# First layer of a four-layer trunk: VectorE in the source's order, the weighting placed behind the next unit's first maxima, the products with v in one piece

## The chip, the cores and the metric

The kernel runs on one core of a Trainium2 chip. The metric is device microseconds of one execution, the median of several runs. All inputs lie in device memory when the time starts, and the output is written back within it.

## What is computed

Four layers over x (256 positions, 1024 channels, float32): a layer normalizes its input, mixes positions, multiplies with a gate, projects and adds a normalized result to its input. The change is in layer 0, "native sparse attention". Its core, cut from the reference:

```python
q, kc, vc, ks, vs, kw, vw, gl, z = split_cols(u @ w_in, A_SPLITS)      # 16 heads, 4 kv heads, 64 wide
kcmp = compress(kc, pos_k, w1_k, w2_k)       # gelu(blk @ w1) @ w2, 15 blocks of 32 positions
vcmp = compress(vc, pos_v, w1_v, w2_v)
p_c = masked_softmax(q @ kcmp - slopes * dist, dist >= 0);   o_c = p_c @ vcmp
p_s = masked_softmax(q @ ks - slopes * dist, causal);        o_s = p_s @ vs
p_w = masked_softmax(q @ kw - slopes * dist, causal);        o_w = p_w @ vw
o = sum(sigmoid(gl) * [o_c, o_s, o_w])       # a gate per head and branch
return (o * silu(z)) @ w_out
```

With 256 positions the selection takes all blocks and the window holds all positions, so the selected and the window branch are both plain causal attention.

## The kernel before, in words

**Split weights.** Products with the weights are done in a reduced float32 format in three matmuls: a weight tile is loaded raw (L83, SyncE's queue, 5 raw buffers), ScalarE copies its high part (L104), VectorE subtracts to get the low part (L106), and TensorE adds high by high, low by high and high by low (L200 to L202, or L260 to L262 in the output projection). `advance` (L69) issues loads and splits as far as buffers allow: 11 split tiles may live at a time, and the low part follows the high part at once in the program.

**Queues.** TensorE's order is that of the source throughout, with other engines ordered by the scheduler, by priorities and a model of the times. In the opening of layer 0 the source orders the other engines too, but not from there on.

**Filling.** A projection is a list of 16 steps of three matmuls, kept in a queue `fq`. `fill` (L208) pops some steps after every slot of attention work, so that TensorE has projection work between the pieces; how many is the rest of the queue less `keep`, over the slots left, rounded up.

**Layer 0 from the compression on.** `compress` (L651) does the first layer of the compression with 64 matmuls (L655), 4 steps of the first q projection behind every quarter; then comes the gelu (L665 to L669), the second layer (L686), and the projections of q for kv heads 1 to 3 (L636 keeps q and its low part, L644) and of the four gate pieces z (L392 to L395, L351, and a split for the output projection, L356 to L360). The 16 heads are 8 units of two; two units make a group that shares a kv head. For each group `cmp_front` (L729) has TensorE score the compressed keys (L736), VectorE reduce, mask, scale and subtract the maximum (L740 to L751), ScalarE take the exponential (L752) and VectorE normalize (L753 to L758); `cmp_back` (L760) transposes. A unit (L767) scores both branches for the first 128 positions in two S tiles (L785, L786), for the last 128 in two more, with two S buffers in all, which the compressed scores use as well. For each tile and branch VectorE adds the mask, takes the row's maximum (L294) and ScalarE the exponential (L296). When all are there, VectorE weights the P tiles with the gate over the sum (L797 to L807); then TensorE transposes them (L301) and multiplies with v (L317, L320), and adds the compressed branch (L819).

**Order of the slots.** `pipeline` (L368) runs the front of a unit against the back of the one before by a pattern, FFBFBBB: compressed scores (first unit of a group), first and second scores, `finish` with the last scores and the weighting, between them transposes of each branch and the products of each branch as slots of their own. Every slot is followed by a fill.

## Time and profile before

| | us |
|---|---|
| median of 3 runs | 581.33 (580.71 to 584.76) |
| the profiled execution | 583.38 |
| its span, first to last instruction | 581.7 |
| TensorE busy in the span | 560.6 (96%) |
| VectorE busy | 420.3 (72%) |
| ScalarE busy | 334.5 (58%) |
| mean granted clock of TensorE | 0.992 of full speed |

In the profile PE is TensorE (its ends are modelled, and matmuls overlap), PEld its weight loads, DVE VectorE, ACT ScalarE, POOL GpSimd, SP SyncE. A tile name stands for all its buffers: S are the score tiles, mm the projections, whi and wlo the split weights, cs the compressed scores, cm and cl their maxima and sums, la the sums of a unit. "Idle before, releaser" is the time that the engine stood still before an instruction and what ended it. The stretch that the change touches runs from about 48 us to the first output projection matmul at 165 us.

### The profile page before, as it was taken

The page shows a single profiled execution, that of the slowest core. Times are in us where ns is not written, and L with a number is a line of the kernel's source. Part 1 is how long each engine was busy: PE and PEld are TensorE (multiplying, and loading weights), DVE is VectorE, ACT ScalarE, POOL GpSimd, SP SyncE. Part 2 cuts the span into 40 slices and gives each one's busy share as a digit, 9 for nine tenths or more (in the row PEclk, how much of TensorE's full clock was granted, in tenths as well). Part 3 has the DMA queues.
Part 4 walks back from the last instruction along what each step waited for, and adds up shares of the span by engine and source line. Part 5 has one row for each costly group of instructions (what it writes and reads, how often), then busy time and mean ns, then how long its engine had stood idle before and what let it go on. Part 6 is the DMA issues. An engine that isn't in the chain of part 4 may idle for free.

```text
span 581.7 us, 10475 instructions
## 1 busy us (share of the span) xinstructions
PE 560.6 (96%) x3930; PEld 496.8 (85%) x3930; DVE 420.3 (72%) x947; ACT 334.5 (58%) x715; POOL 40.7 (7%) x89
## 2 busy tenths in 40 slices
PE   7999987989999999999999999999999999999995
PEld 6998876777788799999988789999987898888984
DVE  5973898887836896777974886768548778888632
ACT  6752787776824475676642474658524765666410
POOL 1900000000000100000420100000001000000000
PEclk9999998999999999999999999999999999999998
DMA  8774925521250596443352568443525683332002
GB/s 296 247 251 146 319 71 190 168 90 44 74 179 4 180 330 231 147 145 126 120 171 73 181 238 302 149 145 110 177 76 181 233 307 137 120 110 74 1 37 73
DMA packets 27779, 90.96 MB, mean 156 GB/s; under 512 B 4560, under 2 KB 5200, under 8 KB 27728
## 3 DMA queue, kind: packets, MB, share of 16 engines
q1 hardware_dynamic: 26144, 86.09, 43.7%
q10 hardware_dynamic: 1584, 4.20, 2.2%
q8 instruction: 31, 0.51, 0.4%
q14 instruction: 20, 0.16, 0.1%
HBM read 89.22 MB, written 1.05 MB: 155 GB/s over the span
## 4 chain that ended last, share of the span: by engine, by line
PE 81%; DVE 8%; issue 4%; ACT 2%; DMA 2%; POOL 1%; SPq 0%; POOLq 0%; DVEq 0%; ACTq 0%
PE mm L200 16%; PE mm L201 14%; PE mm L202 14%; PE mm L262 6%; PE mm L260 6%; PE mm L261 6%; PE pt L301 3%; DVE wlo L106 3%; PE S L311 3%; PE o L317 2%; ACT whi L104 1%; PE o L655 1%; DVE P L294 1%; DMA h<-in_x_dram 1%; PE pt L188 1%
## 5 line engine op out<-in xcount | busy, mean ns | idle before, releaser
L200 PE MATMUL mm<-uth,whi 128*128 128x256 f32 x736 | 219.0, 298 | 0.0
L106 DVE TENSOR_TENSOR wlo<-raw,whi 128x1024 fp32r<-128x1024 f32 (+1 forms) x153 | 182.3, 1207 | 43.4 <-ACT whi L104 42.8
L201 PE MATMUL mm<-utl,whi 128*128 128x256 f32 x736 | 208.5, 283 | 0.0
L202 PE MATMUL mm<-uth,wlo 128*128 128x256 f32 x736 | 208.3, 283 | 0.0
L104 ACT ACTIVATE whi<-raw 128x1024 fp32r<-128x1024 f32 (+1 forms) x153 | 157.0, 1043 | 73.5 <-PE mm L201 38.5
L200 PEld LDWEIGHTS mm<-uth,whi 128*128 128x128 f32 x736 | 140.9, 191 | 15.5 <-issue 14.7
L201 PEld LDWEIGHTS mm<-utl,whi 128*128 128x128 f32 x736 | 141.1, 192 | 0.9
L202 PEld LDWEIGHTS mm<-uth,wlo 128*128 128x128 f32 x736 | 140.9, 191 | 0.0
L260 PE MATMUL mm<-whi,qT 128*128 128x512 f32 x128 | 50.5, 394 | 0.0
L261 PE MATMUL mm<-whi,kT 128*128 128x512 f32 x128 | 49.9, 390 | 0.0
L262 PE MATMUL mm<-wlo,qT 128*128 128x512 f32 x128 | 49.9, 390 | 0.0
L260 PE MATMUL mm<-whi,uth 128*128 128x512 f32 (+1 forms) x112 | 42.6, 380 | 0.0
L262 PE MATMUL mm<-wlo,uth 128*128 128x512 f32 (+1 forms) x112 | 42.1, 376 | 0.0
L261 PE MATMUL mm<-whi,utl 128*128 128x512 f32 (+1 forms) x112 | 42.1, 376 | 0.0
L294 DVE CUSTOM_DVE_ANT_0 P<-S,mask 128x128 f32<-128x128 f32 (+1 forms) x96 | 30.6, 353 | 8.3 <-PE S L786 6.0
L415 ACT ACTIVATE junk<-mm 128x512 bf16<-128x512 f32 x16 | 9.5, 595 | 42.1 <-PE mm L262 42.1
L296 ACT ACTIVATE P<-P,mxa 128x128 f32<-128x128 f32 (+1 forms) x64 | 28.4, 447 | 3.7 <-DVE mxa L294 3.7
L146 ACT ACTIVATE PT<-pt 128x384 f32<-128x384 f32 x58 | 25.8, 483 | 7.5 <-PE pt L301 7.5
L262 PEld LDWEIGHTS mm<-wlo,qT 128*128 128x128 f32 x128 | 24.0, 188 | 5.0
L260 PEld LDWEIGHTS mm<-whi,qT 128*128 128x128 f32 x128 | 24.1, 188 | 4.7
L261 PEld LDWEIGHTS mm<-whi,kT 128*128 128x128 f32 x128 | 24.1, 188 | 4.7
L301 PE MATMUL pt<-ident,P 128*128 128x128 f32 x180 | 27.0, 279 | 0.5 <-DVE P L806 0.4
(207 smaller groups left out, 757.3 us busy)
## 6 DMA issues: line engine op xcount, KB each, us to landing
raw<-in_a_t_dram SPq DMA_DIRECT2D x24, 512.0 KB, 4.8
raw<-in_b_t_dram SPq DMA_DIRECT2D x24, 512.0 KB, 4.6
raw<-in_d_t_dram SPq DMA_DIRECT2D x24, 512.0 KB, 4.5
raw<-in_c_t_dram SPq DMA_DIRECT2D x20, 512.0 KB, 5.2
raw<-in_w_dram SPq DMA_DIRECT2D x8, 512.0 KB, 4.7
raw<-in_a_o_dram SPq DMA_DIRECT2D x8, 512.0 KB, 3.8
raw<-in_b_v_dram SPq DMA_DIRECT2D x8, 512.0 KB, 3.4
raw<-in_b_o_dram SPq DMA_DIRECT2D x8, 512.0 KB, 3.5
```

The source lines that it names most:

```text
L104: ACT.activation(hi, t, AF.Copy)
L106: lo_of = (POOL if on_pool else DVE).tensor_tensor(lo, t, hi.bitcast(F32), op=OP.subtract)
L146: ACT.activation(dst, src, AF.Copy)
L200: PE.matmul(o, sh, mh, start=first, stop=False)
L201: PE.matmul(o, sh, ml, start=False, stop=False)
L202: PE.matmul(o, sl, mh, start=False, stop=last)
L260: PE.matmul(o, sh, wh[:, j, c0:c1], start=k == 0, stop=False)
L261: PE.matmul(o, sl, wh[:, j, c0:c1], start=False, stop=False)
L262: PE.matmul(o, sh, wl[:, j, c0:c1], start=False, stop=k == 7)
L294: DVE.tensor_tensor_reduce(out=P[:, c0:c1], in0=S, in1=mask[:, c0:c1], scale=-slope, scalar=BIG, op0=OP.add, op1=OP.min, accum_out=mx)
L296: ACT.activation(P[:, c0:c1], P[:, c0:c1], AF.Exp, bias=mx, scale=-1.0, accum_out=l)
L301: PE.transpose(pt[:, i, :], P[:, i * 128:(i + 1) * 128], ident)
```

## The change

- From the compression to the end of the attention of layer 0, VectorE runs in the source's order. For that, pieces are moved in the source: `later(n, f)` puts a VectorE step behind n more projection steps (q's low part, the gelu's parts, the gate's product with z, the low part of the gated output).
- The low part of a weight (`low_part`) is no longer issued with the high part. It is kept, and issued one at a time: behind the quarters of the compression, behind the second and the last maxima of each unit, at the latest six projection steps ahead of its use; what is left goes behind the last slot.
- `cmp_front` ends with the exponential; the normalization (`cmp_weights`) goes behind the unit's first maxima. The weighting of a unit (`scale`) goes behind the next unit's first maxima and behind that normalization; the last unit's goes ahead of its transposes.
- The mask additions of the compressed scores become one instruction for both halves, and so do the slope products; the constant tile `dcmp` is laid out for it.
- The products with v of both branches and of the compressed branch become one slot. The order of the slots is written out (`nsa_order`), with 63 instead of 68 slots; the last scores come behind the transposes, the output copy always on ScalarE.

Cut to its core:

```diff
+    def low_parts(n):
+        for i in sorted(low)[:n]:
+            low.pop(i)()
+    def later(n, f):
+        if st["own"]:
+            waiting.append((plan["count"] + n, f))
+        else:
+            f()
+    def overdue(everything=False):
+        while waiting and (everything or waiting[0][0] <= plan["count"]):
+            waiting.popleft()[1]()
...
-                lo_of = (POOL if on_pool else DVE).tensor_tensor(lo, t, hi.bitcast(F32), op=OP.subtract)
+                low[i] = lambda i=i, t=t, hi=hi, lo=lo: low_part(i, t, hi, lo)
+                if not st["own"]:
+                    low.pop(i)()
...
+            for i, at in ((idx[c], 0), (idx[c] + 1, 2)):
+                if k == at and i in low:
+                    low.pop(i)()
...
+    own = ExitStack()
+    own.enter_context(tc.manual_schedule(engines={mybir.EngineType.DVE}))
+    st["own"] = True
...
-        for b in range(2):
-            for c in range(2):
-                DVE.tensor_tensor(cs[:, b, 2 * c:2 * c + 2], cs[:, b, 2 * c:2 * c + 2],
-                                  dcmp[:, c, b, None, :].to_broadcast([128, 2, 15]), op=OP.add)
-        for b in range(2):
-            DVE.tensor_tensor(cs[:, b], cs[:, b], slc[:, g, :, None].to_broadcast([128, 4, 15]), op=OP.mult)
+        pairs = cs.rearrange("p b (c j) n -> p (b c) j n", j=2)
+        DVE.tensor_tensor(pairs, pairs, dcmp.rearrange("p b c n -> p (b c) n")[:, :, None, :]
+                          .to_broadcast([128, 4, 2, 15]), op=OP.add)
+        DVE.tensor_tensor(cs, cs, slc[:, g, None, :, None].to_broadcast([128, 2, 4, 15]), op=OP.mult)
...
         ACT.activation(cs, cs, AF.Exp)
+        CHALF.append(lambda: cmp_weights(g, cs, cs8, cl))
...
         def finish():
             scores_of(1, (1,))
+            low_parts(1)
+            SCALE.append(scale)
...
+        def pvs():
+            pv(0)
+            pv(1)
+            o = t["o"]
+            for j in range(2):
+                PE.matmul(o[64 * j:64 * j + 64, :], vbd[g][:, 2 * i + j, :], PTC[g], start=False, stop=True)
+            evac(ga.oT[:, p, :], o, "a")
+            ga.have_o(p)
+        def first():
+            scores_of(0, (0, 1))
+            for rest in (CHALF, SCALE):
+                if rest:
+                    rest.pop()()
+        def second():
+            scores_of(1, (0,))
+            low_parts(1)
+        def trans_first():
+            if SCALE:
+                SCALE.pop()()
+            trans(0)
+        front = [first, second, finish]
+        back = [trans_first, lambda: trans(1), pvs]
...
+    def nsa_order():
+        units = [nsa_unit(p) for p in range(8)] + [([lambda: None] * 3, None)]
+        order = []
+        for p in range(9):
+            f, b = units[p][0], units[p - 1][1] if p else [lambda: None] * 3
+            if p < 8 and p % 2 == 0:
+                order.append(lambda p=p: cmp_front(p // 2))
+            order += f[:2]
+            if p % 2:
+                order.append(lambda p=p: cmp_back(p // 2))
+            order += [*b[:2], f[2], b[2]]
+            if p == 7:
+                order.append(ga.open)
+        return order
+    gh = run(nsa_order(), ga)
+    low_parts(len(seq))
+    st["own"] = False
+    own.close()
```

## Rows read from the trace of the kernel before

**Rows 1.** Windows: stretch, length, busy (count) by engine, granted clock, DMA share, GB/s.

```profile
60.00:70.00 10.00, 9.60 (x86) 8.77 (x82) 9.22 (x15) 7.62 (x11) 0.00 (x0) 1.00 0.96 357
70.00:89.30 19.30, 17.12 (x130) 14.98 (x131) 18.11 (x70) 15.59 (x45) 0.00 (x0) 1.00 0.35 109
89.30:116.20 26.90, 22.90 (x167) 19.03 (x166) 23.30 (x80) 20.92 (x55) 0.00 (x0) 0.94 0.53 174
116.20:136.50 20.30, 18.63 (x141) 14.72 (x141) 16.29 (x80) 13.97 (x46) 0.00 (x0) 1.00 0.26 92
136.50:156.50 20.00, 19.42 (x149) 15.68 (x148) 16.55 (x81) 16.00 (x51) 1.16 (x4) 1.00 0.21 61
```

**Rows 2.** Waits of TensorE, 60 to 165 us: waiter, releaser, sum, times, longest.

```profile
PE S L785 <- DVE cm L750: 4.3, 2, 2.8
PE S L785 <- DVE cs L740: 2.2, 2, 1.1
```

**Rows 3.** Timeline of TensorE at 98 us: start, duration, operation, idle before.

```profile
97.79 0.77 PE L785 MATMUL S<-kT,qT 128*128 128x512 f32 x1 [2.78 <-DVE cm L750]
```

**Rows 4.** Windows of 2 us at two of the waits.

```profile
98.00:100.00 2.00, 2.00 (x8) 1.81 (x9) 1.31 (x9) 1.65 (x9) 0.00 (x0) 0.50 0.41 166
...
118.00:120.00 2.00, 1.00 (x8) 1.00 (x9) 2.00 (x15) 0.49 (x2) 0.00 (x0) 1.00 0.19 76
```

**Rows 5.** Windows of line 106 alone: VectorE and GpSimd busy (count), clock, DMA.

```profile
89.30:116.20 26.90, 9.57 (x8) 0.00 (x0) 0.94 0.53 174
116.20:136.50 20.30, 2.44 (x2) 0.00 (x0) 1.00 0.26 92
```

**Rows 6.** Groups of VectorE, 60 to 162 us: count, busy, mean ns, idle before.

```profile
L106 DVE TENSOR_TENSOR wlo<-raw,whi 128x1024 fp32r<-128x1024 f32 x23 | 27.6, 1217 | 6.2 <-ACT whi L104 6.0
...
L644 DVE SCALAR_TENSOR_TENSOR qT<-mm,cq,qT 64x512 fp32r<-64x512 f32 x8 | 6.0, 750 | 0.7 <-ACT qT L643 0.5
...
L740 DVE TENSOR_REDUCE cs<-S 128x120 f32<-128x240 f32 x4 | 1.6, 399 | 0.0
...
L751 DVE TENSOR_TENSOR cs<-cs,cm 128x120 f32<-128x120 f32 x4 | 1.1, 280 | 0.0
```

**Rows 7.** Timeline of VectorE at 108 and at 116 us.

```profile
108.10 0.28 DVE L294 CUSTOM_DVE_ANT_0 P<-S,mask 128x128 f32<-128x128 f32 x1
...
108.31 0.20 DVE L797 RECIPROCAL la<-la 128x8 f32<-128x8 f32 x1
108.42 1.17 DVE L106 TENSOR_TENSOR wlo<-raw,whi 128x1024 fp32r<-128x1024 f32 x1
...
116.26 0.19 DVE L797 RECIPROCAL la<-la 128x8 f32<-128x8 f32 x1
116.49 0.17 DVE L800 TENSOR_TENSOR la<-la,gate 128x8 f32<-128x8 f32 x1
116.70 0.29 DVE L806 TENSOR_SCALAR P<-P,la 128x128 f32<-128x128 f32 x1
...
117.17 0.28 DVE L806 TENSOR_SCALAR P<-P,la 128x128 f32<-128x128 f32 x1
```

**Rows 8.** Timeline of TensorE, 116 to 124 us, compressed scores and a product.

```profile
116.26 0.96 PE L736 MATMUL S<-kc,qT 128*128 128x32 f32 x8
...
122.31 0.28 PE L201 MATMUL mm<-utl,whi 128*128 128x256 f32 x1
122.43 0.28 PE L202 MATMUL mm<-uth,wlo 128*128 128x256 f32 x1
...
123.43 0.39 PE L200 MATMUL mm<-uth,whi 128*128 128x256 f32 x1
123.66 0.28 PE L201 MATMUL mm<-utl,whi 128*128 128x256 f32 x1
```

**Rows 9.** Groups of ScalarE, 60 to 162 us.

```profile
L104 ACT ACTIVATE whi<-raw 128x1024 fp32r<-128x1024 f32 x22 | 23.0, 1054 | 10.1 <-PE mm L201 6.2 <-DMA raw<-in_a_t_dram 3.4 <-DMA raw<-in_a_o_dram 0.4
...
L752 ACT ACTIVATE cs<-cs 128x120 f32<-128x120 f32 x4 | 1.2, 293 | 0.0
```

More of the change, by code (lines that the diff above doesn't have):

```diff
@@ L65, in trunk, with low_part @@
         add(n + "_o", *range(8))
-    st = {"load": 0, "split": 0, "next": 0, "held": 0, "parts": 0, "after": [], "most": len(seq)}
-    raw, parts = {}, {}
+    st = {"load": 0, "split": 0, "next": 0, "held": 0, "parts": 0, "after": [], "most": len(seq), "own": False}
+    raw, parts, low = {}, {}, {}
+    waiting = deque()
+    def low_part(i, t, hi, lo):
+        on_pool = i in POOLED
+        lo_of = (POOL if on_pool else DVE).tensor_tensor(lo, t, hi.bitcast(F32), op=OP.subtract)
+        if i == max(POOLED):
+            st["pool"] = lo_of.ins
+        elif not on_pool:
+            st["lo"] = lo_of.ins
+    def low_parts(n):
[9 more added lines that the diff above has]
+            waiting.popleft()[1]()
     def advance(most=len(seq)):
@@ L221, in drain @@
             pop()
+        overdue(True)
     def need(i):
@@ L359, in split @@
                 ACT.activation(hi, g, AF.Copy)
-                DVE.tensor_tensor(lo, g, hi.bitcast(F32), op=OP.subtract)
+                later(3, lambda: DVE.tensor_tensor(lo, g, hi.bitcast(F32), op=OP.subtract))
         def open(self):
@@ L381, in pipeline, with run @@
                 order.append(ga.open)
+        return run(order, ga, keep)
+    def run(order, ga, keep=8):
         plan["slots"], plan["keep"] = len(order), keep
@@ L390, in trunk, with silu_tanh, rest @@
     tanhs = []
-    def silu_tanh(z):
+    def silu_tanh(z, got):
         w = work.tile([128, 2, 256], F32, name="zw", bufs=2)
         tanhs.append(ACT.activation(w, z, AF.Tanh, scale=0.5))
-        DVE.scalar_tensor_tensor(w, w, 1.0, z, op0=OP.add, op1=OP.mult)
-        return w
+        def rest():
+            DVE.scalar_tensor_tensor(w, w, 1.0, z, op0=OP.add, op1=OP.mult)
+            got(w)
+        later(3, rest)
     def out_proj(g, l):
@@ L643, in keep_q @@
             ACT.activation(hi, o[r], AF.Copy, scale=sc)
-            DVE.scalar_tensor_tensor(t["q"][other, hs, :], o[r], sc, hi.bitcast(F32), op0=OP.mult,
-                                     op1=OP.subtract)
+            later(3, lambda r=r, other=other, hs=hs, hi=hi, sc=sc: DVE.scalar_tensor_tensor(
+                t["q"][other, hs, :], o[r], sc, hi.bitcast(F32), op0=OP.mult, op1=OP.subtract))
         ready[g] = plan["count"]
@@ L712, in trunk @@
             compress(q, lp)
+        if q < 3:
+            low_parts(1)
         for f in steps[4 * q:4 * q + 4]:
-            f()
+            fq.append(f)
+            pop()
     for g in range(1, 4):
@@ L816, in pv @@
             pv_pair(o, t["PT", br], v, (br * 256 + g * 64,) * 2, br == 0, False)
[L817 to L830 removed]
+        def pvs():
[13 more added lines that the diff above has]
+            scores_of(1, (0,))
+            low_parts(1)
+        def trans_first():
[4 more added lines that the diff above has]
+        back = [trans_first, lambda: trans(1), pvs]
+        return front, back
+    def nsa_order():
[16 more added lines that the diff above has]
+    own.close()
+    trans = out_proj(gh, 0)
     SLB = slopes_of(8)
```

45 lines of the change are left out of this document (18 added, 27 removed).

## The prediction

> **What bounds the kernel now.** I read the page first: TensorE is busy in 96% of the span, so a gain must come from where TensorE waits, or from TensorE's own work. Then the windows, to find the stretch: from the compressed scores of group 0 (70 us) to the output projection (165 us) TensorE is idle for 19.3 - 17.12 = 2.18 us in the units of group 0, 4.00 in those of group 1, 1.67 in group 2 and 0.58 in group 3; 0.40 lie between 60 and 70 us [rows 1]. VectorE is busy for 18.11 of 19.3 and 23.30 of 26.9 us in the first two groups, 94% and 87%, but for 80% and 83% in the last two [rows 1]. Next the waits: TensorE's waits there are nearly all for a score tile S (two PSUM buffers) that VectorE hasn't read out [rows 2]. The longest shows in the timeline: 2.78 us ahead of the S matmul at 97.79 us [rows 3]. [...]
>
> The idle columns understate the loss. A matmul's record runs 0.28 us, but the next starts after 0.12 [rows 8], so each of some dozen gaps costs 0.16 more than shown (1.9 us). I add about 1.0 us, an estimate, for transposes that wait for their second tile within busy time, and about 1.4 us for the clock (half speed in 2 us and fringes, part of it under the gap) [rows 4]. By group, start to start, I make the loss **2.65, 6.0, 2.65, 1.4, together 12.7 us**, and 0.6 us ahead of 70 us.
>
> **The change part by part.** *Work on VectorE.* Each group has four mask additions of 30 elements and two slope products of 60; they become one and one. Of 120 elements the trace has no such product, so the nearest row prices them, 0.28 us each [rows 6]; a fixed part of 0.1 us for each of four instructions less bounds the gain at 0.4 us a group, nothing bounds it below. I take 0.1. Four of the eight copies of the output go to ScalarE: 1.7 us off VectorE, not off the path. Neither counts by itself.
>
> *Low parts (L106).* Each takes 1.217 us, some 1.14 of it before the next can start [rows 6]. Before, 8 run in group 1 and 2 in group 2 [rows 5]; group 0 has 5 and group 3 has 2. After, one goes behind the second and one behind the last maxima of a unit: 5, 4, 4, 4, and the rest behind the last gate. Group 1 sheds four (4.6 us) of the work that makes VectorE late there; groups 2 and 3 get two more each, 2.3 us against VectorE's idle 4.0 and 3.5 us [rows 1]. Weights come in time: the walk keeps two or more tiles ahead of the projection, and transfers, which wait for a raw buffer that a low part frees, get 2.5 units (over 20 us) each.
>
> *Products in one piece.* From the projection's last matmul (122.43, next possible 122.55) to the next projection matmul at 123.43, the first half takes 0.88 us; 4 of 256 and 4 of 128 columns at 0.12 and 0.06 us would be 0.72, so 0.16 is spent entering and leaving. The projection's first matmul behind it takes 0.23 instead of 0.12 us [rows 8]. Saved: 0.27 us a unit, times 8, **2.2 us**.
>
> *The source's order.* This is the part that can go either way, so I walk it on the two engines. A unit's slots each pop projection steps (0.36 us each): two in the first 26 slots, up to unit 3, one afterwards (97 steps, 8 kept, 63 slots instead of 68). Prices: the reduction of the scores 0.40 us [rows 6]; an instruction that needs the one before starts 0.04 us after its end (0.19, then 0.23 later), an independent one 0.09 us before its end (0.20, then 0.11) [rows 7]. So the chain behind the reduction (add, multiply, maximum, clamp, subtract) is 3 x 0.32 + 0.21 + 0.20 = 1.37 us; four first maxima at 0.22 (0.21 in the row) are 0.88; the softmax weights of the compressed branch (L753 to L758) 1.2; the weighting needs 0.45 for reciprocal and gate and 0.46 per P tile [rows 7].
>
> First unit of a group, one step per slot, time 0 at the compressed scores' first matmul. They end at 0.82 (a record of 0.96 less what overlaps) [rows 8], the reduction runs 1.07 to 1.47, the chain to 2.88. The unit's second S tile waits 0.15 for the reduction; both are scored at 1.8. The first maxima now stand behind the chain: 2.88 to 3.76, the first tile's free at 3.3. TensorE is at the third S tile at 2.17 and starts it at 3.4: **1.25 lost**. Then 0.46 of scores and a step, 4.2. VectorE does the compressed weights to 4.96 and the previous unit's weighting; its first half tile is ready at 5.7, where before the change it was done ahead of the scores: **1.5 lost**, and 0.27 more as the second tile comes late. Sum 3.2 us. With two steps per slot TensorE arrives 0.36 to 0.7 later at both places: 2.05. The second unit of a group has no chain: 0.25.
>
> Group 0 starts with no weighting due, but two pairs of q's low parts (L644, 0.75 us each) and a low part stand ahead of the next maxima [rows 6]: 0.6 at the third tile, 2.1 at unit 1's first two, 0.65 behind, 3.35. At the end, unit 7's weighting stands behind the third gate's product, its use and two gate splits (2.5 us): TensorE has 4.05 us of work there, VectorE needs 5.3, 1.55 with the second tile. **New losses: 3.35 + 2.3 + 3.45 + 3.45 + 1.55 = 14.1 us** instead of 12.7. No gap passes 1.5 us, so I expect no fall of the clock.
>
> *Ahead of 70 us* two low parts leave VectorE's way between the hidden layer and the first scores: 0 to 0.6, I take 0.6 as its waits are for VectorE.
>
> **Sum.** -2.2 - 0.6 - 12.7 + 14.1 = -1.4 us. The profiled execution took 583.38 us (span 581.7), so 582.0; the median of the runs is 581.33, 2.05 lower, so **579.9 us**.
>
> What covers what is free: the output copies on ScalarE, busy 16.00 of 20.0 us in group 3 [rows 1], hide behind the scores; uncovered they would hold the single output buffer for 0.4 us a unit, 3 us. The flushed low parts (five, 5.7 us) lie under 8 us of output projection, whose weights they are only in part; uncovered 1 to 2 us.
>
> [...] The rows differ: 0.23 us start to start chained, 0.11 not [rows 7]. [...]
>
> **The rivals.**
> *A, the forecast (0.50):* the waits of group 1 go, others of like size come at the third S tile and at the first transposes of each group. 579.9, own range 576 to 584.
>
> *B, the waits at the transposes are covered (0.20).* For it: VectorE had 3.5 to 4 us idle in groups 2 and 3 [rows 1], and if projection steps or ScalarE's copies make TensorE later there, the weighting is through when it arrives. Against: it stands behind 3.5 us of VectorE work that begins when TensorE has 1.2 us to do. Gone would be 1.75 twice, 1.4 in group 1 and 1.55 at the end, 6.5 us: 573.4.
>
> *C, chained instructions cost no more than others (0.05).* Eleven links stand ahead of a group's first transposes, 0.13 us each by the rows: 1.4 us in three groups, 0.65 in group 0, 4.9 us: 575.0. The rows speak against it [rows 7]. [...]
>
> *D, slower (0.12):* the compressed weights wait at the head of VectorE's queue for ScalarE's exponential (0.29 us) [rows 9]. It has 0.88 us of cover; a copy of a high part in front of it takes 1.05 [rows 9], and behind the wait stand the weighting, two maxima and a low part, for which transposes and scores wait. It decides where the gap at the transposes grows from 1.5 past what was seen to lower the clock, 2.78 us: then each costs 1.3 more and some 1.4 of clock [rows 3, 4]. At three groups and the end, 10.8 at most, 9 with one clock loss partly covered: 589.
>
> *E, it doesn't do what it says (0.13):* the scheduler's order was already close and new waits equal the old, products included: 581.3.
>
> **How the numbers follow.** A measurement here tells about 1% (5.8 us) from no change. Faster than 575.5: B 0.18, C 0.03, A 0.06, sum 0.27. Slower than 587.1: D 0.10, A 0.01, 0.11. Within: 0.62. The range goes down to B with 1.4 us of unpriced overlap, 572, and up to A with the uncovered copies and half of D, 586; it leaves out half of D and the end of B.
>
> **What would show it.** In the changed trace: waits of TensorE for S named to the chain's instructions gone from group 1, no window below clock 0.9 between 70 and 160 us; gaps of 1 to 1.5 us ahead of the third S tile and of the first transposes of groups 1 to 3; VectorE idle ahead of each unit's first maxima; eight instead of sixteen breaks at the products; out projection's first matmul 1 to 3 us earlier. B is right if the gaps at the transposes stay under 0.4; D if VectorE waits over 1 us for ScalarE's exponential. The forecast is wrong most easily at VectorE's place when the compressed scores end: if it is late there by over 1 us, every later step of the group is.

## The result and the profile after

The changed kernel takes **586.37 us** (median of 16 runs, 584.15 to 588.91), the kernel before on the same chip 583.17 us (16 runs): a ratio of **1.0059, 95% interval 1.0037 to 1.0080**. It is 0.6% slower. That is less than the 1% that I allow for noise, but the interval leaves out 1, and it is the other way than I forecast (579.9); the median lies 0.4 us outside my range (572 to 586). The forecast started from 581.33, the median of three runs, where 16 runs of the kernel before now give 583.17: 1.84 us of the distance between 579.9 and 586.37 is that, and the rest, 4.6 us, is the change itself (-1.4 forecast, +3.2 measured). The profiled execution took 586.66 us with a span of 584.9 us.

The loss lies in one stretch. The timeline gives the first matmul of each group's compressed scores and of the output projection; between them:

| | group 0 | group 1 | group 2 | group 3 and the end | sum | output projection starts |
|---|---|---|---|---|---|---|
| before, us | 19.34 | 26.95 | 20.22 | 28.55 | 95.06 | 165.03 |
| after, us | 23.08 | 22.70 | 20.17 | 33.75 | 99.70 | 168.30 |
| projection steps before / after | 24 / 28 | 25 / 26 | 16 / 14 | 32 / 29 | 97 / 97 | |
| change without the moved steps (0.36 us each) | +2.30 | -4.61 | +0.67 | +6.28 | +4.64 | |

A projection step is three matmuls, 0.36 us; the last row takes out the steps that the new slots moved from one group to another, so that the groups can be compared.

The stretch ahead of group 0 is 1.37 us shorter (68.60 instead of 69.97), which leaves the 3.27 us by which the output projection comes later; the spans differ by 3.2. Most of the 1.37 isn't the change's. The first matmul of the compression, where the changed code begins, already comes 0.98 us earlier (first line before, second after). Ahead of it the profile of the kernel before has a low clock at 12 us and that of the changed kernel hasn't (the windows from 12 to 16 us, in the same order; the granted clock is the third number from the end). Only 0.39 us lie between the compression and group 0.

```profile
48.17 1.95 PE L655 MATMUL o<-raw,qT 128*64 128x256 f32 x16
47.19 1.95 PE L692 MATMUL o<-raw,qT 128*64 128x256 f32 x16
```

```profile
12.00:16.00 4.00, 4.00 (x19) 4.00 (x20) 3.79 (x10) 3.84 (x9) 0.90 (x1) 0.57 1.05 307
12.00:16.00 4.00, 3.74 (x28) 3.43 (x29) 3.79 (x10) 4.00 (x11) 1.03 (x1) 1.00 1.04 264
```

Windows of the changed kernel over the same four groups (columns as in [rows 1]):

```profile
68.60:91.70 23.10, 19.89 (x145) 17.90 (x144) 19.21 (x66) 16.96 (x46) 0.00 (x0) 0.93 0.36 115
91.70:114.40 22.70, 21.23 (x171) 18.00 (x170) 18.86 (x72) 16.51 (x50) 0.00 (x0) 1.00 0.28 93
114.40:134.60 20.20, 17.48 (x136) 13.88 (x134) 18.05 (x70) 16.88 (x54) 0.00 (x0) 1.00 0.33 105
134.60:168.30 33.70, 29.32 (x211) 24.23 (x210) 22.41 (x89) 21.59 (x60) 1.57 (x4) 0.90 0.26 83
```

In group 1 VectorE is now busy for 18.86 of 22.7 us instead of 23.30 of 26.9 [rows 1], and the clock stays at 1.00. In group 0 and in group 3 the clock is what stands out: 0.93 and 0.90, where before it was 1.00 in both.

TensorE's waits from 60 to 165 us (waiter, releaser, sum, times, longest), to be held against [rows 2]:

```profile
PE pt L328 <- DVE P L858: 4.5, 4, 1.7
PE S L833 <- DVE mxa L321: 3.5, 4, 1.1
PE mm L224 <- DVE wlo L72: 2.1, 1, 2.1
PE pt L328 <- ACT PT L168: 1.1, 3, 0.4
```

The waits for the chain (cm, cs) are gone. In their place stand transposes that wait for the weighting, S tiles that wait for the first maxima behind the chain, and two that I had not priced: a projection matmul that waits for a low part, and three transposes that wait for ScalarE to copy the ones before them. The timeline of TensorE at these places (start, duration, operation, idle before):

```profile
77.37 0.39 PE L224 MATMUL mm<-uth,wlo 128*128 128x256 f32 x1 [2.12 <-DVE wlo L72]
...
117.82 0.47 PE L833 MATMUL S<-kT,qT 128*128 128x512 f32 x1 [1.13 <-DVE mxa L321]
...
119.94 0.33 PE L328 MATMUL pt<-ident,P 128*128 128x128 f32 x1 [1.07 <-DVE P L858]
...
158.55 0.61 PE L328 MATMUL pt<-ident,P 128*128 128x128 f32 x3 [1.65 <-DVE P L858]
```

The number in brackets is the idle time by the modelled ends. Below, a wait is mostly given "start to start": the distance from the start of the matmul before, less the 0.12 us that a projection matmul takes anyway. The four waits above are 2.27, 1.28, 1.23 and 1.81 us by that count.

The pair of waits at 117.82 and 119.94 stands again at 137.99 and 140.11 in group 3, as far apart and as long (1.28 and 1.23). What follows each of these waits shows in windows of 2 us:

```profile
78.00:80.00 2.00, 2.00 (x11) 1.96 (x11) 2.00 (x8) 1.27 (x5) 0.00 (x0) 0.55 0.65 236
80.00:82.00 2.00, 2.00 (x13) 2.00 (x12) 1.94 (x10) 1.88 (x6) 0.00 (x0) 0.59 0.76 199
...
120.00:122.00 2.00, 2.00 (x14) 1.57 (x15) 2.00 (x10) 1.12 (x4) 0.00 (x0) 1.00 0.00 0
...
140.00:142.00 2.00, 1.89 (x9) 1.81 (x10) 2.00 (x11) 0.96 (x3) 0.00 (x0) 0.50 0.00 0
...
160.00:162.00 2.00, 2.00 (x11) 1.85 (x10) 0.64 (x2) 1.19 (x3) 0.00 (x0) 0.53 0.02 4
```

In this stretch the clock falls to its lower level (0.50 of full speed) three times: at 78 us, at 139 and at 160. Before, it fell once, at 97 us [rows 4]. Summed over windows of 1 us between 60 and 176 us, what is missing from full clock is 1.71 us before and **5.13 us after**, 1.71 for each fall. Below, "clock loss" is this sum; it bounds what the falls cost from above, as a part of the slow time lies under waits.

That is one execution of each kernel. The mean granted clock of every execution is on record too, and there the two hardly differ: 0.991 on average over 16 executions of the changed kernel (0.987 to 0.995), 0.992 over 94 of the kernel before, which ran beside the experiments (0.983 to 0.998). At the same clock the changed kernel is the slower one: 584.2 to 585.6 us at 0.993 to 0.995 (5 executions), where the kernel before took 580.8 to 583.4 (26). So the profiled pair shows more of a difference in clock than the medians have, and most of the 3.2 us isn't clock.

### The profile page after: what moved, and what is told of

Same layout as the page of the kernel before. It is cut to its first block, busy times and chain, and to the rows that moved or that the text cites. A ratio compares the mean times of both kernels' runs of the same rounds, so it can differ in the third digit from the quotient of the medians.

```text
span 584.9 us, 10456 instructions
## 1 busy us (share of the span) xinstructions
PE 561.1 (96%) x3930; PEld 498.2 (85%) x3930; DVE 420.6 (72%) x927; ACT 335.4 (57%) x719; POOL 41.8 (7%) x89
## 3 DMA queue, kind: packets, MB, share of 16 engines
HBM read 89.22 MB, written 1.05 MB: 154 GB/s over the span
## 4 chain that ended last, share of the span: by engine, by line
PE 81%; DVE 8%; issue 4%; ACT 3%; DMA 2%; POOL 1%; POOLq 0%; DVEq 0%; ACTq 0%; SPq 0%
PE mm L222 15%; PE mm L223 14%; PE mm L224 14%; PE mm L289 6%; PE mm L288 6%; PE mm L287 6%; PE pt L328 4%; PE S L338 3%; DVE wlo L72 3%; PE o L344 2%; ACT whi L129 2%; DMA raw<-in_a_t_dram 1%; PE o L692 1%; PE pt L210 1%; PE mm L519 1%
## 5 line engine op out<-in xcount | busy, mean ns | idle before, releaser
L222 PEld LDWEIGHTS mm<-uth,whi 128*128 128x128 f32 x736 | 141.4, 192 | 14.1 <-issue 13.3
L328 PE MATMUL pt<-ident,P 128*128 128x128 f32 x180 | 28.9, 290 | 5.9 <-DVE P L858 4.5
L321 DVE CUSTOM_DVE_ANT_0 P<-S,mask 128x128 f32<-128x128 f32 (+1 forms) x96 | 29.1, 353 | 7.2 <-PE S L834 4.9
L328 PEld LDWEIGHTS pt<-ident,P 128*128 128x128 f32 x180 | 21.3, 146 | 8.9 <-DVE P L858 3.5
```

What stands on the lines that cost most here:

```text
L222: PE.matmul(o, sh, mh, start=first, stop=False)
L321: DVE.tensor_tensor_reduce(out=P[:, c0:c1], in0=S, in1=mask[:, c0:c1], scale=-slope, scalar=BIG, op0=OP.add, op1=OP.min, accum_out=mx)
L328: PE.transpose(pt[:, i, :], P[:, i * 128:(i + 1) * 128], ident)
```

## The experiments

All ran beside the kernel before. As its median moved between 582.8 and 584.3 us from one set of runs to the next, the ratio is what compares them; a point is 1% of the time of before, 5.8 us. "Stage" is the distance from the first compressed scores to the output projection in the profile.

| kernel | median us | before us | ratio (95% interval) | stage us | clock loss us |
|---|---|---|---|---|---|
| after | 586.37 | 583.17 | 1.0059 (1.0037 to 1.0080) | 99.70 | 5.13 |
| e1 low part earlier | 586.14 | 584.12 | 1.0027 (1.0008 to 1.0046) | 100.32 | 6.83 |
| e2 last weighting earlier | 584.58 | 584.12 | 1.0015 (0.9996 to 1.0034) | 96.35 | 3.42 |
| e3 both | 583.51 | 584.12 | 0.9977 (0.9961 to 0.9992) | 96.38 | 3.42 |
| e4 scheduler's order | 577.33 | 584.12 | 0.9871 (0.9849 to 0.9893) | 88.27 | 0 |
| e5 weighting early | 602.59 | 582.99 | 1.0352 (1.0324 to 1.0381) | 115.43 | 15.37 |
| e7 scores early | 580.18 | 582.99 | 0.9955 (0.9935 to 0.9975) | 95.24 | 3.42 |
| e10 waits filled | 582.71 | 582.99 | 0.9995 (0.9978 to 1.0012) | 96.05 | 1.70 |
| e8 products split | 577.90 | 582.99 | 0.9921 (0.9900 to 0.9942) | 90.23 | 0 |
| e13 weighting first | 580.19 | 584.26 | 0.9932 (0.9911 to 0.9953) | 92.19 | 1.71 |
| e14 maxima first | 582.17 | 584.26 | 0.9961 (0.9945 to 0.9977) | 93.68 | 3.41 |
| e9 nothing deferred | 577.58 | 584.26 | 0.9883 (0.9857 to 0.9909) | 90.30 | 1.71 |
| e16 e14's source, scheduler | 575.72 | 584.26 | 0.9849 (0.9823 to 0.9875) | 87.10 | 0 |
| e17 links between maxima | 580.39 | 583.58 | 0.9945 (0.9927 to 0.9964) | 93.30 | 3.41 |
| e18 e16 with early scores | **574.34** | 583.58 | **0.9843 (0.9816 to 0.9870)** | 85.36 | 0 |
| e19 weights later | 578.80 | 582.78 | 0.9932 (0.9907 to 0.9957) | 92.12 | 1.71 |

My first theory was that two accidents make the loss, the late low part in unit 0 and the late weighting at the end, each with its fall of the clock. The rival: VectorE's fixed order as a whole.

**e1.** A low part more, behind unit 0's first maxima (in `first()`):

```diff
             scores_of(0, (0, 1))
+            if p == 0:
+                low_parts(1)
             for rest in (CHALF, SCALE):
```

> The changed kernel, with one low part more issued behind the first maxima of unit 0, ahead of the compressed weights (its trace: the low part ran at 76.09 us, behind 1.25 us of compressed weights and 1.52 us of q's low parts, and TensorE waited 2.27 us for it at 77.37; then its clock stood at 0.55 and 0.59 for 78 to 82 us). Theory L (the late low part and the fall of the clock behind it are most of the loss): the gap at 77.4 shrinks below 0.5 us, windows 78 to 82 show a clock above 0.9, and the time falls by 2.1 of gap and about 1.7 of clock, to 582.6. Rival O (the loss is VectorE's in-order queue as a whole; a low part put ahead of the weights makes the next maxima late by its own 1.2 us): a gap of 1 to 2 us reappears at the next S tiles, and the time stays within 1 us of 586.4.

Measured: 586.14, ratio 1.0027, an interval that overlaps that of the changed kernel. The 2.12 us wait went, and others of the same sum came. VectorE at that place (timeline), then TensorE's waits for S (60 to 165 us):

```profile
72.71 1.22 DVE L72 TENSOR_TENSOR wlo<-raw,whi 128x1024 fp32r<-128x1024 f32 x1
...
75.09 1.52 DVE L681 SCALAR_TENSOR_TENSOR qT<-mm,cq,qT 64x512 fp32r<-64x512 f32 x2
...
76.64 0.43 DVE L321 CUSTOM_DVE_ANT_0 P<-S,mask 128x256 f32<-128x256 f32 x1
...
```

```profile
PE S L833 <- DVE mxa L321: 5.5, 7, 1.4
```

Seven waits of 5.5 us instead of four of 3.5: in group 0, TensorE lost 0.47, 1.52 and 0.53 us start to start at the next S tiles, 2.52 together, where the low part had cost 2.27. Group 0 itself became 1.36 us shorter (21.72), as its fall of the clock was absent, but in this execution the clock fell in group 2 as well (21.87 instead of 20.17). The late low part was a symptom: VectorE's queue is full there (its timeline shows no wait from 72.5 to 81 us), and whatever comes first makes the rest late.

**e2.** The last unit's weighting directly behind its last maxima:

```diff
             scores_of(1, (1,))
+            if p == 7:
+                scale()
             low_parts(1)
-            SCALE.append(scale)
+            if p < 7:
+                SCALE.append(scale)
```

> The changed kernel, with the weighting of the last unit (2.3 us) issued directly behind its last maxima instead of behind the third gate's product and splits (in its trace TensorE waits 1.81 us at 158.55 for the weighting, and the clock stands at 0.53 and 0.61 from 160 to 164). Theory T (that wait and its clock are a loss of their own): the gap at 158.5 falls below 0.4 us, the clock keeps above 0.9 up to the output projection, and the time falls by 1.5 and about 1.5 us to 583.4. Rival G (the gates that the weighting now delays by 2.3 us are what the output projection waits for): its first matmul comes at the same 168.3 us, and the time stays at 586.4.

Measured: ratio 1.0015, 0.44 points (2.6 us) below the changed kernel. The wait at 158 us and the fall behind it are gone and the output projection starts at 165.67. Theory T holds for this place: the weighting had stood behind the third gate's uses, as this timeline of VectorE in the changed kernel shows.

```profile
155.13 0.68 DVE L430 SCALAR_TENSOR_TENSOR zw<-zw,mm 128x512 f32<-128x512 f32 x1
...
156.48 1.28 DVE L390 TENSOR_TENSOR kT<-oT,qT 128x512 fp32r<-128x512 f32 x2
157.68 0.19 DVE L849 RECIPROCAL la<-la 128x8 f32<-128x8 f32 x1
...
```

**e3.** Both edits, those of e1 and e2.

> Both edits of the two runs before together. Theories L and T: the gains add up, 586.4 - 3.8 - 3.0 = 579.6, and the remaining waits are those at the third S tile and at the first transposes of groups 1 to 3, 1.2 to 1.3 us each. Rivals O and G: 586.4, or the gain of one of the two alone, 582.6 to 583.4.

Measured: 583.51, ratio 0.9977: 0.8 points below the changed kernel, instead of the 6.8 us (1.2%) expected. The end was real, the low part mostly not, so the fixed order as a whole was next to test.

**e4.** VectorE put in order by the scheduler again; all else of the change stays:

```diff
-    own.enter_context(tc.manual_schedule(engines={mybir.EngineType.DVE}))
```

> The changed kernel with VectorE's instructions put in order by the scheduler again, as before the change; slots, deferred low parts, merged additions and products in one piece stay. If the order in the source is what costs (walk: 0.9 + 2.3 in groups 0 and 1, 2.5 in each of groups 2 and 3, 1.8 at the end), the waits at the third S tile and the first transposes go down to what the scheduler's order had before, and the time is 583.2 - 2.2 (products in one piece) = 581.0. If the deferral of the low parts costs, the late low part and the fall of the clock stay: 585 to 587.

Measured: **577.33, ratio 0.9871**. Neither case expected so much. The fixed order costs 1.9 points, 11 us (9.0 by the medians; the stage: 99.70 against 88.27, shorter in every group), and all the rest of the change together gains 1.3%. The clock doesn't fall in the stage. Group 1's window and the timeline of VectorE in group 2 show how the scheduler does it:

```profile
90.90:111.70 20.80, 20.80 (x170) 18.04 (x169) 19.62 (x71) 19.02 (x53) 0.00 (x0) 1.00 0.49 166
```

```profile
113.39 0.29 DVE L321 CUSTOM_DVE_ANT_0 P<-S,mask 128x128 f32<-128x128 f32 x1
...
113.61 0.28 DVE L788 TENSOR_TENSOR cs<-cs,dcmp 128x120 f32<-128x120 f32 x1
113.81 0.28 DVE L321 CUSTOM_DVE_ANT_0 P<-S,mask 128x128 f32<-128x128 f32 x1
...
114.02 0.28 DVE L790 TENSOR_TENSOR cs<-cs,slc 128x120 f32<-128x120 f32 x1
114.21 0.28 DVE L321 CUSTOM_DVE_ANT_0 P<-S,mask 128x128 f32<-128x128 f32 x1
...
```

The links of the chain stand between the first maxima, one of each in 0.40 to 0.42 us (113.39, 113.81, 114.21), so an S tile is read out while the chain goes on, and no link waits for the one before. (The chain is the run of additions, product, maximum, clamp and subtraction on the compressed scores, a link one of its instructions.) In one block, as in the changed kernel, a link takes 0.32 us and a maximum 0.21. Whether this place of the links is what makes the scheduler's order the faster one is not shown here; e17 comes back to it.

**e5.** Back to the weighting ahead of the next unit's scores, in the fixed order (on e3):

```diff
             scores_of(1, (1,))
+            scale()
             low_parts(1)
-            SCALE.append(scale)
```

> Both fixes (e3), and every unit's weighting directly behind its own last maxima, not behind the next unit's first maxima: one part of the change undone, with VectorE still in the source's order. In e3 TensorE lost 1.23 us twice and 0.88 once at the first transposes of an even unit, which wait for this weighting, and 1.28 twice and 0.66 at the third S tile; its clock fell twice (3.4 us). Theory P (the place of the weighting is what costs): the waits at the transposes go (3.3 us), those at the third S tile grow by less than that, for VectorE now waits about 0.6 us for ScalarE's exponential ahead of each weighting; with one fall of the clock less, 583.5 - 3.3 + 1.8 - 1.7 = 580.3. Rival Q (any fixed order that holds the whole chain in one piece costs the same: what leaves one wait comes back in the other): 583.5 or more, with waits of 2 us or more at the third S tile.

Measured: 602.59, on rival Q's side and far beyond it. TensorE's waits (60 to 172 us) and VectorE's timeline in unit 1:

```profile
PE S L833 <- DVE mxa L321: 17.3, 10, 4.2
PE S L833 <- DVE cs L787: 4.6, 3, 3.0
```

```profile
80.27 0.20 DVE L849 RECIPROCAL la<-la 128x8 f32<-128x8 f32 x1 [0.92 <-ACT P L323]
...
82.56 1.22 DVE L72 TENSOR_TENSOR wlo<-raw,whi 128x1024 fp32r<-128x1024 f32 x1
83.69 0.28 DVE L321 CUSTOM_DVE_ANT_0 P<-S,mask 128x128 f32<-128x128 f32 x1
...
```

The weighting waits 0.92 us for ScalarE's exponential, takes 2.3, and the next unit's maxima stand behind it and a low part: waits of up to 4.2 us. The part of the change that puts the weighting behind the next unit's maxima is worth 19 to 22 us in a fixed order (602.59 against e3's 583.51 by the medians, 3.75 points by the ratios); a part of that is clock (15.37 against 3.42). What it is worth with the scheduler wasn't tried.

**e7.** Compressed scores of groups 1 to 3 ahead of the products with v instead of behind them (on e3):

```diff
+            if p == 0:
+                order.append(lambda: cmp_front(0))
...
+            order += [*b[:2], f[2]]
+            if p % 2 and p < 7:
+                order.append(lambda p=p: cmp_front(p // 2 + 1))
+            order.append(b[2])
```

> Both fixes (e3), and the compressed scores of groups 1 to 3 one slot earlier, ahead of the products with v of the unit before the last, so that TensorE has 2.1 us of products and a step to do while VectorE runs the chain. Theory W (the waits come from a chain of 1.8 us that begins when TensorE has 1.35 us of other work; with cover they go): 0.66 and twice 1.28 at the third S tile and 0.88 and twice 1.23 at the first transposes fall below 0.3 each, about 5 us, and the clock keeps above 0.9 (3.4 us): 583.5 - 8.4 = 575 (at least below 578). Rival Q (VectorE is late as a whole, the place of the scores doesn't matter): the waits move to other tiles, 582 to 584.

Measured: 580.18, half a percent below before. Against e3 that is 0.2 points (1.3 us; 1.1 in the stage), with intervals that overlap, where 8.4 us were expected. The third S tiles lost 0.17, 1.22 and 0.78 us instead of 0.66, 1.28 and 1.29; the transposes still 0.87, 1.22 and 1.23. The chain got its cover, but the weighting still stood behind the compressed weights.

**e10.** Ten spare matmuls where TensorE only waits (on e3):

```diff
+    def spare():
+        junk = ps.tile([128, 256], F32, name="o", bufs=1)
+        for _ in range(10):
+            PE.matmul(junk, uT[0][:, 0, 0:128], uT[1][:, 0, :], start=True, stop=True)
...
+            if p in (4, 6):
+                spare()
             scores_of(1, (0,))
...
+            if p in (3, 5):
+                spare()
             trans(0)
```

> Both fixes (e3), and ten more matmuls of 256 columns, whose product nothing reads, ahead of the third S tile and ahead of the first transposes of groups 2 and 3 (40 in all, some 1.2 us each time), where TensorE only waits in e3 (1.28 and 1.23 us, then a clock of 0.50 in 119 to 123 and 140 to 143 us, 3.4 us lost by the windows). Theory C (the falls of the clock are a loss of their own, caused by these waits): TensorE starts the tile behind each wait at the same distance as before, the clock keeps above 0.95, and the time falls by 3 to 3.4 us, to 580.3. Rival N (the slow stretches only lie where VectorE is the bound anyway, so that their length costs nothing): the time stays at 583.5 or grows.

Measured: 582.71, ratio 0.9995: not faster than e3 (0.9977). At the two places the edit did what it should. Timeline of TensorE in group 2, then the window behind:

```profile
116.22 1.12 PE L779 MATMUL o<-utl,uth 128*128 128x256 f32 x8
117.27 0.47 PE L838 MATMUL S<-kT,qT 128*128 128x512 f32 x1
...
118.15 1.35 PE L779 MATMUL o<-utl,uth 128*128 128x256 f32 x10
119.39 0.33 PE L328 MATMUL pt<-ident,P 128*128 128x128 f32 x1
```

```profile
118.60:120.60 2.00, 2.00 (x16) 1.66 (x15) 1.93 (x10) 1.36 (x2) 0.00 (x0) 1.00 0.00 0
```

The S tile and the transposes stand 2.12 us apart, as in e3 (117.01, 119.13), and the clock holds. Group 2 took 20.17 us against 21.57 in e3. But in group 3 a new wait of 0.86 us came, and in this execution the clock fell at 80 us in group 0, where the kernels don't differ. Nor was that only this execution: over the 12 of each kernel the mean clock is 0.995 here and 0.991 in e3, and still the time isn't lower. So on the time rival N stands: holding the clock with spare matmuls gained nothing as a whole. Whether that is VectorE's pace or the spare matmuls themselves isn't shown.

What a single fall costs shows in groups that are the same in two kernels. Group 2 took 20.17 us in the changed kernel, where the clock held, and 21.14 (e2) and 21.57 us (e3) with one fall; group 3 took 29.31 us in e2, where it held, and 30.37 in e3, where it fell; group 0 took 21.74 us in e3 and 22.95 in e10. That is **1.0 to 1.4 us a fall**. (In e1 the low stretch in group 2 was twice as long, 6.83 - 3.42 = 3.41 us of clock loss, and cost 1.7.) The windows of group 0 in e3 and e10 and of group 3 in e2 and e3 (ends rounded to 0.1 us):

```profile
69.10:90.90 21.80, 18.84 (x146) 16.53 (x144) 18.96 (x66) 16.35 (x44) 0.00 (x0) 1.00 0.36 122
68.20:91.10 22.90, 20.08 (x143) 17.89 (x143) 18.94 (x66) 17.05 (x47) 0.00 (x0) 0.93 0.36 116
...
136.40:165.70 29.30, 26.57 (x212) 21.76 (x211) 22.57 (x89) 21.51 (x60) 1.15 (x4) 1.00 0.27 95
135.10:165.50 30.40, 27.64 (x211) 23.16 (x210) 22.75 (x89) 21.59 (x60) 1.15 (x4) 0.94 0.27 92
```

The executions of the kernel before agree: by a straight-line fit over each set of runs they take 1.2 to 1.4 us longer where the mean clock is 0.003 lower, which is one fall (1.71 of 582 us).

**e8.** On e4, a projection step between the two halves of the products:

```diff
             pv(0)
+            if len(fq) > 8:
+                pop()
             pv(1)
```

> The scheduler's order on VectorE (e4), with a projection step between the two halves of a unit's products with v, as before the change. The prediction took 0.27 us a unit for the break, 2.2 us for eight (seven have a step left to put there): 577.3 + 1.9 to 2.2 = 579.4. If the break costs nothing (the step's first matmul is as late behind one piece as behind two halves): 577.3.

Measured: the stage grew by 1.96 us, the ratio by 0.5 points (2.9 us, with an uncertainty of 1.8). The output projection comes only 0.53 us later, but e4's profile had lost 1.43 us ahead of the compression, with a fall of the clock at 13 us. The timelines give the price directly. From the start of the projection's last matmul to the start of the next one, the products in one piece take 2.24 us in e4, the two pieces in e8 1.01 and 1.59. Less 0.12 for the one matmul more that is counted, and with 0.1 that the first matmul behind the extra piece takes longer, that is 0.34 us a unit, 2.4 us in seven units. My term of 2.2 us for the products in one piece stands.

**e13.** On e3, the weighting ahead of the compressed weights:

```diff
-            for rest in (CHALF, SCALE):
+            for rest in (SCALE, CHALF):
```

> Both fixes (e3), VectorE in the source's order, and behind a unit's first maxima the previous unit's weighting comes ahead of the compressed weights instead of behind them: two lines of the order change places. In the changed kernel the compressed weights (1.2 us, and up to 0.5 of waiting for ScalarE's exponential) stand between the first maxima and the weighting that the first transposes wait for. Theory W (each wait is set by what stands just ahead of it in VectorE's queue): the waits at the first transposes of groups 1 to 3 (0.88, 1.23, 1.23) fall below 0.3, those at the third S tile (0.66, 1.28, 1.29) stay; 583.5 - 2.7, and with them at least one of the two falls of the clock (1.0 to 1.7 us): 579.5. Rival Q (VectorE's queue is late as a whole): the waits come back at the next S tiles or transposes, 582.5 to 584.

Measured: 580.19, 0.45 points below e3 (about 2.6 us). No first transpose of groups 1 to 3 waits for the weighting any more, and the third S tiles keep their 0.66, 1.29 and 1.29. Theory W holds for the transposes: what stands just ahead in VectorE's queue sets the wait.

**e14.** On e3, another fixed order. The chain behind the reduction goes into a list `LINKS`, and:

```diff
             scores_of(0, (0, 1))
-            for rest in (CHALF, SCALE):
-                if rest:
-                    rest.pop()()
+            if SCALE:
+                SCALE.pop()()
...
             scores_of(1, (0,))
+            if LINKS:
+                LINKS.pop()()
             low_parts(1)
...
             scores_of(1, (1,))
+            if CHALF:
+                CHALF.pop()()
```

> Both fixes (e3), VectorE in a fixed order, but another one in the first unit of a group: the reduction of the compressed scores, the first maxima, the previous unit's weighting, the second maxima, then the chain (additions to subtraction), a low part, the last maxima, and only then the compressed weights. Theory W: third S tile and first transposes no longer wait (0.93, 0.66, 0.88, 1.28, 1.23, 1.29, 1.23 in e3, 7.5 us), no fall of the clock is left (3.4 us), and a fixed order is as fast as the scheduler's: 583.5 - 7.5 - 3.4 + about 1 at the next tiles = 573.5, with e4's 577.3 as the upper end. Rival Q (a fixed order loses as such, since VectorE then waits for ScalarE at its head): 580 or more, with VectorE waits for ScalarE of over 3 us between 70 and 160 us.

Measured: 582.17, a miss of 8.7 us, and by the ratio level with e3. The third S tiles of the first units hardly wait, but those of the *second* units now lose 0.99, 1.51 and 1.22 us, as the compressed weights and a low part stand ahead of their maxima, and group 0 loses 2.12 and 1.20 and the clock. VectorE's longest waits for ScalarE were 3.8 us (q's low parts) and 2.5, which the rival had named.

**e9.** On e4, nothing deferred:

```diff
-    st["own"] = True
```

> The scheduler's order (e4), with nothing deferred any more: each low part is issued with its high part, and the uses of gates and of q's parts at once, as before the change; slots, merged additions, products in one piece and the later weighting stay. Theory D (moving low parts out of groups 0 and 1 gains, as the prediction had it: four parts, 4.6 us of VectorE in group 1): the waits for S in group 1 come back, 577.3 + 2 to 4 = 580. Rival: with the scheduler the place in the source doesn't matter: 577.3.

Measured: 577.58, ratio 0.9883, the same as e4 within the intervals. The profile shows both sides: group 1 takes 24.49 us instead of 20.81, with waits of 0.83 and 1.16 us for VectorE and a fall of the clock, as theory D said, and group 3 gives 1.4 of it back (26.84 instead of 28.24). In time nothing can be told.

**e16.** e14's source with e4's scheduler:

```diff
-    own.enter_context(tc.manual_schedule(engines={mybir.EngineType.DVE}))
```

> The source order of e14 (first maxima, weighting, second maxima, chain, weights behind the last maxima) with the scheduler's order on VectorE (e4). In e4 the waits left are 0.6 at the third S tile of group 0, 1.0 and 1.5 at transposes in groups 0 and 2 and 1.3 at the end. If the scheduler follows the source's places as priorities, the weighting comes earlier and 1.5 to 2.5 us of these go: 575 to 576; if it orders by readiness alone: 577.3.

Measured: 575.72, ratio 0.9849, in the range expected of a scheduler that follows the source's places. But the interval overlaps that of e4 (0.9871), so this isn't shown. The same source in a fixed order (e14) takes 6.5 us more.

**e17.** e13's order, with a link of the chain behind each first maximum. In `scores_of`:

```diff
                             t["mx"][:, x:x + 1], t["l"][:, x:x + 1])
+                    if LINKS:
+                        LINKS.pop(0)()
```

> The order of e13 (fixed, both fixes, weighting ahead of the compressed weights), with the links of the chain between the first maxima: reduction, maximum, addition, maximum, product, maximum, group maximum, maximum, clamp, subtraction. In the scheduler's trace (e4) a pair of link and maximum takes 0.41 us so; in one block they take 0.32 and 0.21. Theory B (blocks of chained instructions cost): the first S tile of a unit is read out about 0.8 us earlier, so the waits at the third S tile (0.93, 0.66, 1.29, 1.29) fall to 0.5 or less, and the one fall of the clock behind them (1.7 us) goes: 580.2 - 3 to -4 = 576.5. Rival F (a fixed order loses as such): 579.5 or more, the waits stay or come back elsewhere.

Measured: 580.39, no gain over e13. The named waits did go: 0.93, 0.66, 1.29 and 1.29 us at the third S tiles became nothing, nothing, nothing and 0.37. At the first transposes of groups 1 to 3, 0.50, 0.85 and 0.85 came back, and in group 0 this stands ahead of the second maxima (VectorE's timeline):

```profile
72.67 1.22 DVE L72 TENSOR_TENSOR wlo<-raw,whi 128x1024 fp32r<-128x1024 f32 x1
74.49 0.28 DVE L806 TENSOR_REDUCE cl<-cs 128x8 f32<-128x120 f32 x1 [0.60 <-ACT cs L800]
...
75.75 1.51 DVE L681 SCALAR_TENSOR_TENSOR qT<-mm,cq,qT 64x512 fp32r<-64x512 f32 x2
77.29 0.43 DVE L321 CUSTOM_DVE_ANT_0 P<-S,mask 128x256 f32<-128x256 f32 x1
```

Their S tile's last matmul had started at 72.01. TensorE lost 1.94 and 1.51 us there, and the clock fell for seven microseconds. Theory B is right on the block and wrong on the time.

**e19.** e17, with the compressed weights behind the second maxima and q's low parts two steps later:

```diff
-            for rest in (SCALE, CHALF):
-                if rest:
-                    rest.pop()()
+            if SCALE:
+                SCALE.pop()()
...
             scores_of(1, (0,))
+            if CHALF:
+                CHALF.pop()()
...
-            later(3, lambda r=r, other=other, hs=hs, hi=hi, sc=sc: DVE.scalar_tensor_tensor(
+            later(5, lambda r=r, other=other, hs=hs, hi=hi, sc=sc: DVE.scalar_tensor_tensor(
```

> The fixed order of e17 with the compressed weights (1.25 us, behind a wait for ScalarE of 0.6) put behind the second maxima instead of ahead of them, and q's low parts (1.5 us) two steps later. If a fixed order loses only through work that stands ahead of maxima and that nothing waits for yet: the two waits of group 0 (1.94 and 1.51 us in e17) fall below 1 us together, the fall of the clock at 78 us goes (3.4 us by the windows, some 2 in time), and the time is 580.4 - 2.5 - 2 = 576 to 577.5, as fast as the scheduler's order (e4, 577.3). If a fixed order loses as such: 579.5 or more, with new waits of VectorE for ScalarE at its head.

Measured: 578.80, the lowest of the fixed orders, by the ratio (0.9932) level with e13, and between the two cases. The second maxima came at 73.71, and a wait of 2.84 us appeared at the third ones, behind the same weights, a low part and q's low parts.

**e18.** e16 with the diff of e7.

> The scheduler's order with the source of e16, and the compressed scores of groups 1 to 3 one slot earlier (as in e7). If the place of the scores still limits, the waits for S in e16 that remain (0.86 and 0.33 behind the compressed weights, 0.3 and 0.2 at third tiles) go: 574.5. If VectorE's order already covers them: 575.7, within 1 us.

Measured: **574.34, ratio 0.9843**, 1.6% faster than before and, by the ratios, 2.1% faster than the changed kernel. It is the lowest time of all, but the ratio is that of e16 within the intervals, so whether the place of the scores still counts isn't settled. The output projection starts at 155.60 us instead of 165.03.

```profile
155.60 0.40 PE L287 MATMUL mm<-whi,qT 128*128 128x512 f32 x1
```

## Why the prediction was wrong, point by point

*"No gap passes 1.5 us, so I expect no fall of the clock": wrong, and the step that failed.* The sum counted 1.4 us of clock in the loss before (12.7) and nothing in the loss after (14.1). In the profile the clock fell three times, and two of the falls came behind single waits longer than 1.5 us: 2.27 us for the low part and 1.81 at the end. The third came with the pair of 1.28 and 1.23 in group 3, each below 1.5. I had read one wait of 1.09 us without a fall (at 119.00 in the kernel before, the line below; the clock stays at 1.00 there) and one of 2.78 with one [rows 3, 4] as a bound on single gaps. Such a pair is enough at times: of nine (groups 2 and 3 of after, e1, e2 and e3, and group 2 of e7) six brought a fall, once (e1, group 2) with the first wait already. Rival D had this price, but tied it to single gaps beyond what was seen. With 1.0 to 1.4 us a fall (e10), the three cost 3.0 to 4.2 us.

```profile
119.00 0.39 PE L785 MATMUL S<-kT,qT 128*128 128x256 f32 x1 [1.09 <-DVE cs L740]
```

*How much of the miss that is.* With 0.54 us a group off for the products, I had forecast changes of +0.16, -4.24, +0.26 and +3.06 us for the four groups; measured, without the moved steps, are +2.30, -4.61, +0.67 and +6.28. The difference is 5.40 us in sum (+2.14, -0.37, +0.41, +3.22), most of it in groups 0 and 3, where the falls are. The falls make 3.0 to 4.2 of it in this execution. Over all executions the clock is about the same as before (0.991 and 0.992), so there the step failed in another way: the 1.4 us of clock that the sum took as won were not won. The rest of the 4.6 us is time at equal clock.

*The walk of the waits: close where it looked, but not complete.* At the third S tile I had 1.25 and find 1.28; at the first transposes 1.5, find 1.23; with two steps per slot, where I let TensorE arrive 0.36 to 0.7 later, 0.65 and 0.87 are left. It left out the transposes that wait for ScalarE's copy of the ones before: 0.42, 0.58 and 0.58 us start to start in groups 1 to 3, 1.6 us together. In group 2 that copy stands behind the high part of a weight on ScalarE (1.05 us at 128.56). Which waits make up the rest at equal clock isn't traced.

*"Weights come in time": wrong on the place, right on the size.* I had 2.1 us of wait at unit 1's first S tiles; TensorE waited 2.27 us for a low part instead, a projection step that reached its tile before the walk had put out its low part. e1 turned the one into the other.

*The end: 1.55 forecast, 1.81 found*, but with a fall of the clock, and e2 shows that it was avoidable.

*Products in one piece, 2.2 us: right* (e8). *Ahead of 70 us, 0.6:* 0.39 found between the compression and group 0; the other 0.98 us of the 1.37 lie ahead of the change.

*The rivals.* A's mechanism is what happened, with the clock on top. B didn't: transposes waited 0.87 to 1.23 us in groups 1 to 3. C didn't either: a link behind the instruction it needs costs 0.32 us here (115.82 to 116.14 in the changed kernel), one between independent maxima 0.20 (113.61 to 113.81 in e4). Of D, VectorE's wait for the exponential was 0.48 us in group 0 alone, but its clock came. E came nearest in time (no change), but not by its reason: the scheduler's order with the rest of the change takes 577.3 us.

*What I hadn't seen at all.* I compared the fixed order with the order before and found them alike. The other parts of the change were a gain that the scheduler would have kept (e4, -1.3%), and the fixed order took it back (+1.9 points). That is the larger lesson of the runs, and it is shown by one line of edit. Some edits within the fixed order took a wait away for good (e2 and e13, 2.6 us each), most moved it (e1, e7, e14, e17, e19). The ratios are 0.9932 to 1.0352 with a fixed order and 0.9843 to 0.9883 with the scheduler, 0.9921 in e8, which takes a part of the change back. Whether a fixed order that copies the scheduler's would be as fast wasn't tried.

## What to carry to other kernels

VectorE was busy for 19.21 of 23.10 us in group 0 of the changed kernel, and with its order fixed, instructions that nothing waited for yet delayed the ones behind them (in e17 the second maxima, whose S tile's last matmul had started at 72.01, came at 77.29, behind a low part, the compressed weights and q's low parts). A change that also fixes an order should be tried once without that part, as e4 does in one line. An edit that takes one wait away has to be judged by the stage, not by the wait: e17 put the links of the chain between independent maxima, the waits it aimed at went, and the time stayed. Price a wait of TensorE not only by its length but by what it may do to the clock (1.0 to 1.4 us a fall here), and look at the clock of many executions before giving it the blame for a difference between two profiles.

## What the runs showed of the hardware

The clock fell after waits shorter than I had thought: after one of 1.65 us idle (158.55 in the changed kernel), one of 2.12 us (77.37 there), and in six of nine cases after two of about 1.1 us idle each. The same waits don't always bring a fall: the pair left the clock at 1.00 in the other three cases, and in group 0 waits of 0.5, 1.5 and 0.5 us start to start brought a fall in e7 and e10 and none in e1, e3 and e13. One fall cost 1.0 to 1.4 us where a group can be compared with and without it.
